# Order edges for side work on TensorE, and new VectorE durations in the account that paces it

## The chip, the cores and the metric

One core of a Trainium2 chip runs the whole kernel. The metric is the device time of one execution in microseconds; a kernel's time is the median over several runs. Engines are named as in the profile: PE is TensorE's matmuls and PEld its weight loads, DVE is VectorE, ACT is ScalarE, POOL is GpSimd, SP is SyncE, which issues most DMAs.

## The reference

One layer of a streaming encoder, on 2048 prompt frames and 64 sample frames, 1024 channels, all in fp32:

```python
h = rms_norm(x, p['norm1_g']) * (1 + sc1) + sh1
z = h @ p['w_in']
glu_a, glu_b, q, k, v, g_conv, g_attn = jnp.split(z, offs, axis=-1)
u = glu_a * jax.nn.sigmoid(glu_b)
conv_out, conv_state = conv_module(u, conv_hist, ...)   # 31 taps, LayerNorm, swish, projection
q, k = rms_norm per head
o = attend(q, k, v, p['rel_bias'])                       # own chunk of 64 and 8 before, 8 heads
attn_out = o @ p['w_attn_out']
merged = jax.nn.sigmoid(g_conv) * conv_out + jax.nn.sigmoid(g_attn) * attn_out
x = x + gt1 * (merged @ p['w_o'])
h2 = rms_norm(x, p['norm2_g']) * (1 + sc2) + sh2
gate, up = jnp.split(h2 @ p['w_ffn_in'], 2, axis=-1)
x = x + gt2 * ((jax.nn.silu(gate) * up) @ p['w_ffn_out'])
```

`sh1`, `sc1`, `gt1` and so on come from a projection of a conditioning vector. The outputs are both parts' frames, the convolution's last 30 rows, and new keys and values.

## The kernel before

Every fp32 product is done as three matmuls on values split into a high and a low part (`mm3`: high by high, high by low, low by high). ScalarE makes the high part, VectorE or GpSimd the low one by subtraction.

**Two phases.** The first (to about 1211 us in the trace) runs over four blocks of some 512 frames. For each block, in the order `q`, GLU columns 0, `k`, GLU columns 1, `v`, GLU columns 2 and 3, `g` (16 columns of gates), TensorE does the main line of products: `qkv`, `glu`, `gates`. The second phase runs over three token blocks with the merge, the output projection, the residual and the feed-forward part.

**Side work.** Beside the main line runs work that is written as Python generators and held in lanes: `norm_tile` and `cached_kv` (the next block's normalised and transposed input), `qk_rows` (norm and transposition of q and k rows), `attend` (one head of attention: scores `sc`, VectorE's row maximum, ScalarE's exponential, transpositions `ptp`, products `po`), `conv_norm` (the convolution's LayerNorm, whose means are matmuls `pm`) and `convolve` (30 VectorE steps a channel tile). Their order of precedence is `[norm_lane, work, attn, tail, conv]`. A generator yields the time at which its next step may be emitted.

**The account.** `Meter` wraps each engine. Every instruction that is traced adds an assumed duration to `Stream.load` of its engine; nothing of it is measured while the kernel is built. TensorE's sum is the clock. After each product (`mm3`, `mm2`) at least 500 ns of that clock on, `tick` lets each lane emit a step if the time that it yielded has come and no engine is further ahead of TensorE than the lane's room: `CONV_ROOM = 2000` ns of VectorE for the convolution, `ATTN = {"dve": 3000, "act": 4000}` for attention, 2500 ns between the score tiles of one head. The waits are built from `stream.when(...)`, the account of the engine whose result is needed, plus lags such as `PE_LAG = 400`, `MEAN_LAG = 10000` (before `conv_norm`, except in the last block) and `KN_LAG = 5000`.

**Drains.** At fixed places a lane is emptied, whatever its times say: `conv.drain()` and `tail.drain()` at GLU stage 0 of each block (so the norm of a block must be through by then), `norm_lane.drain` of a tile ahead of its q product, and `attn`, `conv` and `tail` at the end of the first phase. At the eleventh gate of the last block the convolution is drained too.

**Emission and issue.** Emission fixes the order in which instructions are traced. The framework's scheduler then orders each engine's queue by what it reckons ready, so that an instruction can be issued ahead of one traced before it. `tc.issue_after(x)` gives all instructions of x's engine that are traced in its block an order edge behind x: issue order alone, no wait for x to end. Before the change it is used on VectorE, around single steps.

**The second phase** has lanes of its own (`turns`, `work`), made after the first ones are gone; its weight handling (`Weights`) uses the same account, for when a buffer is given up and whether GpSimd or VectorE makes a low part.

All instructions go through one helper line of `Meter`, L105, so the profile's rows are told apart by tile names.

Of the kernel before, what the change touches and what calls it, by code (L numbers as in the profile page):

```python
# [87 lines left out]
class Meter:  # L88


    def __init__(self, engine, name, stream):
        self.engine, self.name, self.stream = engine, name, stream

    def __getattr__(self, op):
        f = getattr(self.engine, op)
        if op == "dma_start":
            return f

        def run(*args, **kw):
            out = kw.get("out", args[0] if args else None)  # L100
            n = 1
            for d in out.shape[1:]:
                n *= d
            self.stream.add(self.name, op, n, args, kw)
            return f(*args, **kw)  # L105

        return run


class Lane:  # L110

# [4 lines left out]
    def add(self, gen):  # L118
        self.gens.append([gen, 0.0, {}])
# [6 lines left out]
        self.step(self.gens[-1])  # L126

    def step(self, entry):
        try:
            got = next(entry[0])  # L130
        except StopIteration:
            self.gens.remove(entry)
            return
        entry[1], entry[2] = got if isinstance(got, tuple) else (got, {})
# [28 lines left out]
class Stream:  # L163
# [1 line left out]


    def __init__(self):
        self.lanes, self.later, self.last = [], [], 0.0
        self.load = {"pe": 0.0, "dve": 0.0, "act": 0.0, "pool": 0.0}

    def add(self, name, op, n, args, kw):
        if name == "pe":
            x = args[1]
            if op == "transpose":
                ns = 128 / 1.2
            elif x.dtype == F32:
                ns = max(n, 64) / (2.4 if "tile_position" in kw else 0.6)
            else:
                ns = (n if n >= 256 else 512) / 2.4
        elif name == "act":  # L180
            ns = 220 + 0.83 * n
        elif name == "pool":
            ns = 260.0 * n if ALU.pow in args else 60 + 2.25 * n
        else:
            fast = op in ("tensor_scalar", "tensor_copy")
            ns = 75 + n * (8.3 if op == "reciprocal" else 0.75 if fast else 1.04)
        self.load[name] = max(self.load[name], self.load["pe"]) + ns

    def full(self, room):
# [401 lines left out]
def streaming_layer(ctx: ExitStack, tc: tile.TileContext, I, O):  # L591
    nc = tc.nc
    stream = Stream()
    pe, dve, act, gps = (
        Meter(e, n, stream) for e, n in ((nc.tensor, "pe"), (nc.vector, "dve"), (nc.scalar, "act"), (nc.gpsimd, "pool"))
    )
# [959 lines left out]
    attn = Lane(ATTN, ATTN_NS, wide=2)  # L1556
    conv, tail = Lane({"dve": CONV_ROOM}, burst=4), Lane({})
    stream.lanes = [norm_lane, work, attn, tail, conv]

    hh = wk.tile([P, KT, QB + SMP], F32R, tag="hh", name="hh")  # L1560
    hl = wk.tile([P, KT, QB + SMP], F32R, tag="hl", name="hl")
# [224 lines left out]
    for s, (lo, hi) in enumerate(CBLOCKS):  # L1786
# [214 lines left out]
        def up(f, ops, at):  # L2001
# [12 lines left out]
            if not f:  # L2014
                z = bank("y")
                step(z, "s3", "t3", True, False)
            step(y, "s2", "t2", f < EARLY, False)
            rest_of_late(1)
            u2 = piece("t1", "u2")[:, :half]
# [4 lines left out]
            if f:  # L2024
                z = bank("y")
                step(z, "s3", "t3", True, False)
# [185 lines left out]
```

## Time and profile before

| | |
|---|---|
| median of 3 runs | 3004.08 us (2999.04 to 3005.18) |
| the profiled execution | 2997.87 us, span 2995.2 us |
| TensorE busy | 2910.2 us, 97% |
| weight loads | 2595.7 us, 87% |
| VectorE busy | 2030.2 us, 68% |
| ScalarE, GpSimd | 1324.2 us, 942.1 us |
| granted TensorE clock, mean | 0.991 |
| end of the first phase | 1211 us |

The page's first part gives each engine's busy time. A row of the waits reads: who waited, for whom, total us, times, longest. A row of the timeline reads: start, duration, engine, line, operation, output and inputs, shapes, count, and in brackets the idle time before it and what ended it. A row of the windows reads: from and to, length, each engine's busy time with its count of instructions, the granted clock as a share of full speed, the DMA engines' busy share and GB/s. In names of tiles, `sc`, `ptp`, `po` are attention, `pm` the convolution's norm, `pt` transpositions, `ps` the main line's products, `y<-u,wd,y` a convolution step.

### The profile page before, as it was taken

To read this page: it belongs to the slowest core of one execution; us is meant where nothing else is said; L and a number is where in the kernel's file an instruction comes from. 1 tells how busy PE (TensorE), PEld (TensorE's weight loads), DVE (VectorE), ACT (ScalarE), POOL (GpSimd) and SP (SyncE) were. 2 spreads that over 40 slices of the span, in tenths; PEclk is the share of its full clock that TensorE was granted. 3 is DMA by queue.
4 is the path that set the end of the run, shared out by engine and by line. 5 is a ranking of instruction groups with operands and counts; after the bars stand their busy time and mean duration, and the time that the engine had idled before them with its cause. 6 is when DMAs were issued, how large, how long until landed. Compare 5 with 4: busy or idle time off the path is not lost.

```text
span 2995.2 us, 44652 instructions
## 1 busy us (share of the span) xinstructions
PE 2910.2 (97%) x16199; PEld 2595.7 (87%) x16199; DVE 2030.2 (68%) x3661; ACT 1324.2 (44%) x2375; POOL 942.1 (31%) x597
## 2 busy tenths in 40 slices
PE   7999989999999999989999999999999999999999
PEld 4888867887888788888999999999999898999998
DVE  5878688677866895577777755556566757366567
ACT  3344642463366257464444345434444244333332
POOL 1200120011011102355455433256656441333333
PEclk9999999999999999999999999999999999999999
DMA  8888889878987788886444786446556955355545
GB/s 299 272 290 270 290 263 304 277 251 273 306 283 248 251 268 289 267 287 235 146 153 161 253 282 230 138 141 204 189 177 213 360 197 190 117 168 176 169 155 186
DMA packets 487017, 690.95 MB, mean 231 GB/s; under 512 B 38420, under 2 KB 316808, under 8 KB 486797
## 3 DMA queue, kind: packets, MB, share of 16 engines
q1 hardware_dynamic: 469749, 662.07, 66.9%
q10 hardware_dynamic: 17048, 26.04, 2.4%
q8 instruction: 127, 2.08, 0.3%
q14 instruction: 93, 0.76, 0.1%
HBM read 503.79 MB, written 184.19 MB: 230 GB/s over the span
## 4 chain that ended last, share of the span: by engine, by line
PE 84%; DVE 8%; DMA 4%; issue 1%; POOL 1%; ACT 1%; SPq 0%; ACTq 0%; DVEq 0%; POOLq 0%
PE ps L105 55%; PE pd L105 14%; PE pw L105 6%; DVE y L105 3%; PE sc L105 2%; PE po L105 2%; PE ptp L105 2%; PE pt L105 1%; POOL r L105 1%; DVE wlo L105 1%; PE pa L105 1%; DMA wlo<-w_dfi_l 1%; DMA out<-acc 0%; DMA g_d<-gate 0%; DMA kk<-k_d 0%
## 5 line engine op out<-in xcount | busy, mean ns | idle before, releaser
L105 POOL TENSOR_TENSOR wlo<-wst,whi 128x1024 fp32r<-128x1024 f32 (+1 forms) x167 | 382.7, 2295 | 566.6 <-ACT whi L105 491.5
L105 PE MATMUL ps<-t,whi 128*128 128x384 f32 (+1 forms) x2112 | 506.0, 323 | 10.2 <-DVE t L105 6.2
L105 PE MATMUL pd<-whi,hid 128*128 128x512 f32 x1356 | 440.3, 391 | 2.7 <-DVE acc L105 2.7
L105 ACT ACTIVATE whi<-wst 128x1024 fp32r<-128x1024 f32 (+1 forms) x271 | 265.0, 982 | 376.8 <-PE ps L105 126.1
L105 PEld LDWEIGHTS ps<-t,whi 128*128 128x128 f32 x2112 | 369.7, 188 | 19.7 <-DVE t L105 7.8
L105 PE MATMUL ps<-b,whi 128*128 128x384 f32 (+1 forms) x1584 | 380.1, 326 | 4.4 <-DVE pt L105 2.4
L105 DVE SCALAR_TENSOR_TENSOR y<-u,wd,y 128x512 f32<-128x512 f32 (+1 forms) x480 | 369.2, 772 | 7.7
L105 PE MATMUL ps<-hh,whi 128*128 128x512 f32 (+2 forms) x992 | 364.8, 368 | 0.0
L105 PE MATMUL ps<-hl,whi 128*128 128x512 f32 (+2 forms) x992 | 347.7, 351 | 0.0
L105 PE MATMUL ps<-hh,wlo 128*128 128x512 f32 (+2 forms) x992 | 347.2, 350 | 0.0
L105 PE MATMUL ps<-t,wlo 128*128 128x384 f32 (+1 forms) x1056 | 340.1, 322 | 0.0
L105 DVE TENSOR_TENSOR acc<-acc,pd 128x512 f32<-128x512 f32 x440 | 289.7, 683 | 65.9 <-PE pd L105 62.3
L105 PEld LDWEIGHTS pd<-whi,hid 128*128 128x128 f32 x1356 | 254.5, 188 | 56.9 <-DVE acc L105 5.1
L105 PEld LDWEIGHTS ps<-b,whi 128*128 128x128 f32 x1584 | 277.4, 189 | 6.1 <-DVE pt L105 2.7
L105 PE MATMUL pd<-wlo,hid 128*128 128x512 f32 x700 | 273.8, 391 | 0.0
L105 PE MATMUL ps<-b,wlo 128*128 128x384 f32 (+1 forms) x792 | 256.6, 324 | 0.0
L105 ACT ACTIVATE pr<-pr,sm 128x640 f32<-128x640 f32 (+3 forms) x272 | 199.9, 746 | 121.6 <-DVE sm L105 117.7
L105 PEld LDWEIGHTS ps<-hh,wlo 128*128 128x128 f32 x992 | 188.3, 190 | 23.6 <-issue 1.2
L105 PEld LDWEIGHTS ps<-hh,whi 128*128 128x128 f32 x992 | 188.8, 190 | 20.0 <-issue 4.1
L105 PEld LDWEIGHTS ps<-hl,whi 128*128 128x128 f32 x992 | 189.2, 191 | 16.0 <-issue 2.5
L105 POOL TENSOR_TENSOR r<-t,mhalf 128x1 f32<-128x1 f32 (+3 forms) x68 | 82.0, 1208 | 378.2 <-DVE t L105 367.1
L105 PEld LDWEIGHTS ps<-t,wlo 128*128 128x128 f32 x1056 | 198.6, 188 | 0.9
(220 smaller groups left out, 5664.7 us busy)
## 6 DMA issues: line engine op xcount, KB each, us to landing
whi<-w_din_h SPq DMA_DIRECT2D x72, 512.0 KB, 5.6
wlo<-w_din_l SPq DMA_DIRECT2D x72, 512.0 KB, 7.6
wst<-sum_d SPq DMA_DIRECT2D x132, 256.0 KB, 3.0
wmod<-in_w_ada SPq DMA_DIRECT2D x48, 512.0 KB, 6.2
sum_d<-ws SPq DMA_DIRECT2D x88, 256.0 KB, 2.2
wst<-in_w_ffn_in SPq DMA_DIRECT2D x84, 256.0 KB, 3.2
wst<-in_w_in SPq DMA_DIRECT2D x40, 512.0 KB, 5.9
wst<-in_w_ffn_in SPq DMA_DIRECT2D x37, 512.0 KB, 5.5
```

Source lines behind the costliest of these rows:

```text
L105: return f(*args, **kw)
```

## The change

Two things are changed. First, `Meter` notes the last TensorE instruction traced (`stream.latest`), and `Lane.step` runs each step of a generator of the five lanes of the first phase inside `issue_after` of it. `Lane.stream` is set for those five lanes alone; lanes made later have none and run as before. Second, the account's VectorE durations are replaced: instead of 75 ns and 1.04 ns an element (0.75 for `tensor_scalar` and `tensor_copy`, 8.3 for `reciprocal`), each kind has a base and a rate of its own.

```diff
             self.stream.add(self.name, op, n, args, kw)
-            return f(*args, **kw)
+            one = f(*args, **kw)
+            if self.name == "pe":
+                self.stream.latest = one
+            return one
...
 class Lane:
+
+    stream = None
...
     def step(self, entry):
+        one = self.stream.latest if self.stream is not None else None
         try:
-            got = next(entry[0])
+            with self.stream.tc.issue_after(one.ins) if one is not None else nullcontext():
+                got = next(entry[0])
...
-            fast = op in ("tensor_scalar", "tensor_copy")
-            ns = 75 + n * (8.3 if op == "reciprocal" else 0.75 if fast else 1.04)
+            base, each = {
+                "tensor_scalar": (300, 0.45), "tensor_copy": (300, 0.45), "reciprocal": (75, 8.3),
+                "scalar_tensor_tensor": (220, 1.04), "tensor_tensor_reduce": (230, 1.04),
+            }.get(op, (150, 1.04))
+            ns = base + each * n
...
     stream.lanes = [norm_lane, work, attn, tail, conv]
+    stream.tc = tc
+    for lane in stream.lanes:
+        lane.stream = stream
```

`either`, which chooses between VectorE and GpSimd for a few operations, keeps the old figures, and its margins (`TT_LESS = 9e9`) leave them all on VectorE.

More of the change, by code (lines that the diff above doesn't have):

```diff
@@ L167, in __init__ @@
     def __init__(self):
-        self.lanes, self.later, self.last = [], [], 0.0
+        self.lanes, self.later, self.last, self.latest = [], [], 0.0, None
         self.load = {"pe": 0.0, "dve": 0.0, "act": 0.0, "pool": 0.0}
```

## The prediction

> **What bounds the kernel now.** I read the page first, then who waited for whom on TensorE (PE) up to the second phase, then busy times stage by stage.
>
> ```profile
> span 2995.2 us, 44652 instructions
> PE 2910.2 (97%) x16199; PEld 2595.7 (87%) x16199; DVE 2030.2 (68%) x3661; ACT 1324.2 (44%) x2375; POOL 942.1 (31%) x597
> ```
>
> TensorE is the bound: 85 us of the span are idle on it. A change of order can win those, and what the clock loses around them, and no more; VectorE (DVE) has a third of the span free. TensorE's waits between 60 and 600 us (total, times, longest):
>
> ```profile
> PE pm L105 <- POOL s L105: 9.2, 1, 9.2
> PE sc L105 <- DVE sm L105: 8.6, 6, 3.2
> PE ptp L105 <- ACT pr L105: 7.9, 5, 4.0
> PE pt L105 <- DVE kn L105: 2.9, 2, 1.8
> ```
>
> All four are side work: `pm` is the convolution's norm, `sc` and `ptp` are attention, `pt<-kn` the turning of q and k rows. Together 28.6 us. Columns below: window, PE, PEld, DVE, ACT, POOL busy, granted clock, DMA. The windows are: k and v rows and the GLU columns of the second block, the same of the third block, the third block's gates, and the last block's gates.
>
> ```profile
> 400.00:525.00 125.00, 116.89 (x624) 90.27 (x613) 104.40 (x197) 42.87 (x88) 9.32 (x11) 0.96 0.88 289
> 682.00:796.00 114.00, 112.61 (x626) 91.73 (x628) 89.72 (x153) 33.43 (x60) 11.88 (x11) 1.00 0.90 299
> 796.00:926.00 130.00, 130.00 (x741) 110.17 (x734) 91.83 (x184) 75.06 (x135) 13.16 (x14) 1.00 0.86 275
> 1068.00:1211.00 143.00, 140.41 (x752) 118.96 (x750) 101.43 (x199) 95.25 (x165) 21.92 (x14) 1.00 0.82 262
> ```
>
> The third block has almost no stall, the second block loses 8.1 us to idle time in the same stages. So there is something to win in the first 600 us, and something to lose after them.
>
> **Part one: pinning.** During a step of a side lane, each TensorE instruction gets an order edge behind the last TensorE instruction traced before the step. It is no wait, and instructions of other engines and DMAs get no edge. It binds only where the scheduler had moved side work ahead; the lanes of the second phase get none. The clear place in the trace:
>
> ```profile
> 502.63 8.40 DMA whi<-w_din_h
> ```
> ```profile
> 508.03 0.74 PE L105 MATMUL sc<-kk,q 128*128 128x320 f32 x4
> 511.95 1.43 PE L105 MATMUL sc<-kk,q 128*128 128x320 f32 x4 [3.17 <-DVE sm L105]
> 514.31 1.43 PE L105 MATMUL sc<-kk,q 128*128 128x320 f32 x4 [0.93 <-DVE sm L105]
> 516.67 1.44 PE L105 MATMUL sc<-kk,q 128*128 128x320 f32 x4 [0.93 <-DVE sm L105]
> 519.04 0.80 PE L105 MATMUL ps<-hh,whi 128*128 128x512 f32 x1
> ```
>
> Four score tiles of one head stand together, the last three ahead of the gates' first matmuls, and each waits until VectorE has emptied the bank of the one before. The step that issues a score tile was emitted between gate matmuls, so the edges spread them out again. That takes away 3.17 + 0.93 + 0.93 = 5.03 us, but not all of it is won: the gates' weights, issued at 502.63, land 8.40 later at 511.03, and the score tiles before end at 508.77, so TensorE stands 2.3 us either way. Net -2.7 us. The clock:
>
> ```profile
> 113.00:115.20 2.20, 0.38 (x3) 0.11 (x2) 0.91 (x2) 0.00 (x0) 1.26 (x1) 1.00 0.00 0
> 115.30:118.70 3.40, 3.40 (x14) 2.81 (x13) 1.98 (x6) 3.04 (x7) 1.65 (x1) 0.51 0.42 91
> 508.70:511.30 2.60, 0.07 (x1) 0.00 (x0) 2.42 (x5) 0.00 (x0) 0.21 (x1) 1.00 1.05 406
> 511.30:521.50 10.20, 7.70 (x29) 4.82 (x29) 9.90 (x22) 6.57 (x12) 0.00 (x0) 0.50 0.45 158
> ```
>
> After the stall the clock is at one half for 10.2 us, 7.70 of them busy, which costs 7.70 / 2 = 3.9 us. A wait of 1.8 us (2.20 less 0.38 busy) at 113 was followed by 3.4 us at one half, or 1.7 us lost, so a 2.3 us stall keeps about that much: -2.2 us of the clock at best; I take -1.5, and -0.8 for the other score waits of the table (8.6 less 5.03). Part one: **-5 us**. Ends: 0 (the scores come to wait elsewhere) and -10 (the weights' landing moves too).
>
> [...]
>
> **Part two: VectorE's account.** The account paces the lanes: convolution steps are emitted while VectorE is at most 2000 ns ahead of TensorE, attention at 3000, and each `yield` of a time waits for VectorE's count. Durations (busy, mean ns, idle before) up to 1211 us:
>
> ```profile
> L105 DVE SCALAR_TENSOR_TENSOR y<-u,wd,y 128x512 f32<-128x512 f32 x360 | 268.4, 749 | 6.1
> L105 DVE SCALAR_TENSOR_TENSOR y<-u,wd,y 128x606 f32<-128x606 f32 x120 | 100.8, 844 | 1.6
> L105 DVE TENSOR_TENSOR pl<-ptp,ph 128x512 fp32r<-128x512 f32 x128 | 86.6, 687 | 58.4 <-ACT ph L105 57.2
> L105 DVE CUSTOM_DVE_ANT_0 pr<-sc,bias 128x640 f32<-128x640 f32 x96 | 78.5, 818 | 24.1 <-PE sc L105 23.7
> ```
>
> Old formula against new: a convolution step 607 and 752 ns (705 and 850 at 606 wide), a 512 wide tensor_tensor 607 and 682, a row maximum 741 and 896, a 128 wide tensor_scalar 171 and 358. Those of the rows are the mean durations now. But as a rate a duration counts too much, since the next instruction starts before the last one ends:
>
> ```profile
> 361.71 0.69 DVE L105 TENSOR_TENSOR hl<-h,hh 128x512 fp32r<-128x512 f32 x1
> 362.32 0.68 DVE L105 TENSOR_REDUCE ssq<-sq 128x8 f32<-128x512 f32 x1
> ...
> 511.07 0.82 DVE L105 CUSTOM_DVE_ANT_0 pr<-sc,bias 128x640 f32<-128x640 f32 x1
> 511.81 0.08 DVE L105 DVE_READ_ACCUMULATOR2_ANT sm<- 128x1 f32 x1
> ```
>
> Start to start it is 0.61 and 0.74 us, the old 607 and 741. So the old account was right for these and short for the convolution; the new one is right for the convolution and long for the rest. In the third block's gates the program's formulas give VectorE 81.8 us before and 99.0 us after (44 steps of +145, 44 tensor_tensor of +75, 20 maxima of +155, 16 small tensor_scalar of +187), against 121.0 us of TensorE: shares of 0.68 and 0.82. The trace has 91.83 of 130.00, or 0.71. The lanes will believe in a VectorE fuller than it is, and emit side work later. Where that lands, place by place:
>
> First 600 us: attention and q/k rows, emitted later, find their inputs ready more often, and fewer convolution steps stand ahead of a row maximum. Of the table's 28.6 us, `pm` (9.2) and the three score waits (5.03) are counted elsewhere; 14.4 us remain, with some 4 us of half clock (an estimate, two stalls at the 1.7 us of the row at 113). I take well under half: **-7 us**. Ends 0 and -18.
>
> The norm of the first block. Its convolution needs, in the new account, 105.8 us; what the other VectorE work leaves in the stages up to the gates (each stage's TensorE time less that work) is 47.6, so 58.2 go into the gates, where 60.1 of 119 us are free. It ends 115 us into them instead of 71 (the same sum with the old formulas gives 68). Then come the norm's fixed 10 us and 46 us of its small part, and the deadline is 29 us after the gates: the next block's first GLU stage drains the lane at once. Today this happens with the large part alone:
>
> ```profile
> 379.36 2.60 POOL L105 TENSOR_TENSOR s<-s,ln 128x512 f32<-128x512 f32 x2 [9.34 <-ACT ln L105]
> 384.84 2.08 PE L105 MATMUL pm<-s,ones 128*128 128x512 f32 x2 [9.24 <-POOL s L105]
> 385.93 1.42 PE L105 MATMUL ps<-hh,whi 128*128 128x512 f32 x1
> ```
>
> Then half of the small part and the three sums on POOL (2.60 / 2 = 1.3 us each, 3.9) join that chain, in front of `pm` and of the columns. 3.9 for the sums and 4 for the rest of the small part (an estimate: somewhat under half of the 9.24 us that one such chain costs today): **+8 us**. Ends 0 (columns are issued in between) and +14.
>
> The turn into the next block (the next q rows, window as above):
>
> ```profile
> 338.00:374.00 36.00, 33.54 (x166) 25.65 (x165) 23.65 (x71) 20.50 (x53) 6.54 (x5) 1.00 0.83 263
> ...
> 926.00:959.00 33.00, 33.00 (x181) 27.96 (x180) 25.25 (x62) 22.09 (x45) 6.33 (x5) 1.00 0.61 186
> ```
>
> The first turn loses 2.5 us today, the last nothing. In blocks two and three 47 convolution steps instead of 41 are left for the gates, 35 us at a free share of 0.56: they end 63 us into the gates instead of 36, and the norm behind them runs on into the turn, where it shares VectorE with the next block's tiles, whose eight small tensor_scalar are priced 1.5 us more per tile. I take 1 us for each of three turns: **+3 us**, ends 0 and +9.
>
> The end of phase one. Attention of the last block ends with the last gate:
>
> ```profile
> 1208.67 0.27 PE L105 MATMUL po<-pl,vv 128*128 128x128 f32 x1
> 1211.41 0.87 PE L105 MATMUL ps<-cin,whi 128*128 128x320 f32 x2 [2.47 <-DVE o_p L105]
> ```
>
> A head has 4 maxima and some 6.5 tensor_tensor in its chain: +1.1 us on the 33 us that a head takes in the account with two in flight, 3.4%, or 4 us over the account's 131 us of this stage, and up to 9 where the other head's are in the way too. That much is left for the drain when no gate matmul covers it; `DVE pl` alone has 5 x 0.69 there, and the convolution's norm, 12 us later by the same sum as above, adds its tail. **+7 us**; ends 0 (the steps' grain swallows it) and +12.
>
> Phase two has no pinned lane; the residual tiles are emitted later, and drains wait for more. Its waits on such tiles today, in the same view from 1211 us on:
>
> ```profile
> PE ps L105 <- DVE t L105: 6.8, 5, 2.4
> ...
> PE pw L105 <- ACT xn L105: 2.7, 1, 2.7
> ```
>
> Three sections of about 1 us: **+3 us**, ends -5 and +8. No DMA is added or removed; weight loads and stores are queued on SP by the same events, later by tenths of a microsecond, which I price at nothing since the third block shows TensorE uncovered for 0.0 us in its gates.
>
> **Sum.** -5 - 7 + 8 + 3 + 7 + 3 = +9 us. The profiled execution took 2997.87 us (2995.2 of span and 2.7 around it), 6.2 under the median of 3004.08, so +9 gives 3007 beside it and **3013 us** as the median. One measurement of this kernel can tell about 0.2%, or 6.0 us, from no change: faster is under 2998.1, slower over 3010.1.
>
> **Rivals.** (a) Faster: the smoothing wins and the drains do not cost. What decides is the order at the first drain: if the scheduler issues the columns at 385.93 ahead of a `pm` that it knows to be late, the +8 is 0, and with -5, -7 to -18 and half of the last three terms (+6) the time is 3004 - 6 to 3004 - 17, with 2992 in the middle. For it: 28.6 us of waits of just the kind that a longer account removes. Against it: the scheduler left TensorE 9.24 us before `pm` with columns ready behind. (b) The change does not do what it says: few edges bind, since most side work already stands behind the main line, and later emission shifts stalls without changing their sum: -5 + 5 = 0, 2999 to 3009 us. For it: only the scores near 512 us show a cost of running ahead. (c) A worse slow case, inside the forecast: all upper ends at once, 14 + 9 + 12 + 8 = +43 with nothing won, 3047; they share causes, but hardly all.
>
> **Chances.** Slower, as summed: 0.41, its own range 3010 to 3040. Faster (a): 0.35. Same (b): 0.24. The range over all cases leaves out about a tenth on each side: of the fast case the times below 2982, where nearly all of -5 and -18 would have to come with no drain paid; of the slow one those above 3038, about four fifths of the upper ends' 43.
>
> **What would show it.** Right: score tiles no longer grouped before 519; convolution steps of the first block still running near 338 us (end of the gates); the wait of `pm` on POOL grown beyond 9.2 us; attention's `po` after the last gate matmul with more than 2.47 us before `ps<-cin`. Wrong: `pm` not waiting at all, phase one ending before 1205 us, or new stalls inside the third block's gates, for which I charged nothing.

## The result, and the profile after

The changed kernel takes 3082.34 us in the median (3080.84 to 3083.43); the kernel before, run beside it, 3004.63 us. The ratio is 1.0267, with a 95% interval of [1.0252, 1.0281]: slower by some 78 us, where 9 were forecast. The profiled execution's first lines:

```profile
span 3079.1 us, 44630 instructions
PE 2925.9 (95%) x16199; PEld 2607.3 (85%) x16199; DVE 2143.7 (70%) x3786; ACT 1324.7 (43%) x2375; POOL 719.6 (23%) x472
```

TensorE has the same 16199 instructions and 15.7 us more busy time (2910.2 before); its mean granted clock is 0.981 instead of 0.991, so I read the 15.7 us as clock lost around stalls. The rest of the 83.9 us between the two spans is idle time: 153.2 instead of 85.0. VectorE has 125 instructions more and GpSimd 125 fewer. That is something the diff does not say in words, and it becomes important below. Who TensorE waited for, over the whole span (total, times, longest):

```profile
PE pm L105 <- POOL s L105: 28.7, 4, 14.9
PE ps L105 <- DVE t L105: 14.9, 6, 9.8
PE sc L105 <- DVE sm L105: 13.1, 11, 4.5
PE ptp L105 <- ACT pr L105: 9.9, 7, 4.9
```

The four kinds of the forecast's first list are all there (`pt<-kn` with 5.0 us stands just below these rows), and none of them is smaller than before. To see where time went, take three instants that both traces have: the first column matmul after the first drain (`ps<-hh,whi` behind `pm`), the last gate matmul, and the first matmul of the second phase (`ps<-cin`).

| stretch | before | after | difference |
|---|---|---|---|
| start to the columns behind the first drain | 385.9 | 406.7 | +20.8 |
| from there to the last gate matmul | 822.1 | 827.2 | +5.1 |
| last gate matmul to phase two | 3.4 | 29.0 | +25.6 |
| phase two | 1783.8 | 1816.2 | +32.4 |

An instant also moves with the side work that was done ahead of it, so the first row has to be read with the matmuls in it, before and after:

```profile
0.00:385.93 385.93, 345.47 (x2149) 295.15 (x2149) 277.59 (x564) 172.65 (x363) 46.95 (x60) 0.97 0.85 284
```
```profile
0.00:406.71 406.71, 342.12 (x2101) 293.33 (x2102) 270.76 (x536) 162.07 (x336) 47.24 (x60) 0.92 0.81 267
```

The changed kernel has 48 matmuls fewer behind it at that instant, 24.1 us more idle time (64.6 and 40.5) and a lower clock, so up to there it has lost more than the 20.8 us of the table. Of the idle time 19.4 us more lie at the drain itself (28.7 from 373.5 us on, 9.2 from 374 us on before) and 3.9 in the turn ahead of it.

The first drain, in TensorE's timeline of the changed kernel; it answers to the single wait of 9.24 us before:

```profile
388.33 0.69 PE L105 MATMUL pm<-s,ones 128*128 128x64 f32 x2 [14.86 <-POOL s L105]
390.96 0.69 PE L105 MATMUL pm<-s,ones 128*128 128x64 f32 x2 [1.94 <-POOL s L105]
397.49 2.07 PE L105 MATMUL pm<-s,ones 128*128 128x512 f32 x2 [5.84 <-POOL s L105]
405.63 2.08 PE L105 MATMUL pm<-s,ones 128*128 128x512 f32 x2 [6.07 <-POOL s L105]
406.71 1.42 PE L105 MATMUL ps<-hh,whi 128*128 128x512 f32 x1
```

All four means of both parts' norms (64 columns and 512 columns wide) stand there. What they wait for is in VectorE's queue, and behind it in GpSimd's:

```profile
376.45 11.45 DVE L105 SCALAR_TENSOR_TENSOR y<-u,wd,y 128x606 f32<-128x606 f32 x13
```
```profile
387.99 0.29 POOL L105 TENSOR_TENSOR s<-s,y 128x64 f32<-128x64 f32 x1 [9.21 <-DVE y L105]
```

Thirteen convolution steps in one run of 11.45 us: the convolution itself had not ended when the drain came.

The end of phase one and the first merge, TensorE:

```profile
1233.94 0.39 PE L105 MATMUL ps<-hh,wlo 128*128 128x512 f32 x1
...
1262.89 0.56 PE L105 MATMUL ps<-cin,whi 128*128 128x320 f32 x2 [1.40 <-DVE o_p L105]
...
1280.00 0.90 PE L105 MATMUL ps<-cin,whi 128*128 128x320 f32 x2 [9.80 <-DVE t L105]
```

And by windows (length, busy times of PE, PEld, DVE, ACT, POOL, granted clock, DMA): the stretch between last gate and phase two, and phase two, with phase two of the kernel before under it.

```profile
1234.40:1262.89 28.49, 18.52 (x88) 14.16 (x86) 16.19 (x29) 16.48 (x30) 5.93 (x4) 0.76 0.34 98
1262.89:3079.10 1816.21, 1761.68 (x9688) 1634.16 (x9688) 1255.13 (x2064) 753.25 (x1291) 571.96 (x326) 0.99 0.60 197
```
```profile
1211.41:2995.20 1783.79, 1755.35 (x9688) 1630.05 (x9688) 1136.40 (x1928) 749.60 (x1283) 796.65 (x450) 1.00 0.60 200
```

Behind the last gate stand 88 matmuls of attention; TensorE is idle for a third of that time and has a clock of 0.76. In phase two TensorE does the same 9688 matmuls, but VectorE is busy 118.7 us longer and GpSimd 224.7 us shorter. The groups that make the low parts of weights say why; GpSimd before, then both engines after (count, busy, mean ns, idle time before them):

```profile
L105 POOL TENSOR_TENSOR wlo<-wst,whi 128x1024 fp32r<-128x1024 f32 (+1 forms) x167 | 382.7, 2295 | 566.6 <-ACT whi L105 491.5
```
```profile
L105 POOL TENSOR_TENSOR wlo<-wst,whi 128x1024 fp32r<-128x1024 f32 (+1 forms) x101 | 238.6, 2365 | 659.6 <-ACT whi L105 499.9
L105 DVE TENSOR_TENSOR wlo<-wst,whi 128x1024 fp32r<-128x1024 f32 (+1 forms) x180 | 214.6, 1198 | 139.1 <-ACT whi L105 127.7
```

`Weights.split` gives a low part to VectorE when GpSimd's account is more than `BEHIND` = 4000 ns ahead of TensorE's. GpSimd's account waits for ScalarE's and that for VectorE's, so VectorE's longer durations push GpSimd's up too (so the code reads; no run takes it apart). Over all low parts of phase two the emission has 165 on GpSimd and 306 on VectorE after, 290 and 181 before: VectorE, believed slower, gets some 125 pieces more to do.

### The profile page after: what moved, and what is told of

The parts are those of the page before. It is cut to its first block, busy times and chain, and to the rows that moved or that the text cites. A ratio compares the mean times of both kernels' runs of the same rounds, so it can differ in the third digit from the quotient of the medians.

```text
span 3079.1 us, 44630 instructions
## 1 busy us (share of the span) xinstructions
PE 2925.9 (95%) x16199; PEld 2607.3 (85%) x16199; DVE 2143.7 (70%) x3786; ACT 1324.7 (43%) x2375; POOL 719.6 (23%) x472
## 4 chain that ended last, share of the span: by engine, by line
PE 48%; DVE 2%; DMA 1%; issue 1%; ACT 1%; POOL 0%; SPq 0%; DVEq 0%; POOLq 0%; ACTq 0%
PE ps L105 30%; PE pd L105 14%; PE pw L105 4%; DVE wlo L105 1%; ACT whi L105 0%; DVE acc L105 0%; DMA wst<-in_w_attn_out 0%; DMA cin<-c_d 0%; DVE pd L105 0%; DMA wst<-in_w_ffn_in 0%; POOL acc L105 0%; POOL ws L105 0%; DVE t L105 0%; DVE pw L105 0%; PE pt L105 0%
## 5 line engine op out<-in xcount | busy, mean ns | idle before, releaser
L105 POOL TENSOR_TENSOR wlo<-wst,whi 128x1024 fp32r<-128x1024 f32 (+1 forms) x101 | 238.6, 2365 | 659.6 <-ACT whi L105 499.9
L105 DVE TENSOR_TENSOR wlo<-wst,whi 128x1024 fp32r<-128x1024 f32 (+1 forms) x180 | 214.6, 1198 | 139.1 <-ACT whi L105 127.7
L105 PEld LDWEIGHTS ps<-hh,whi 128*128 128x128 f32 x992 | 189.5, 191 | 22.5 <-issue 3.1
```

Of the source, the lines that this page charges most:

```text
L105: one = f(*args, **kw)
```

## The experiments

The theory after the traces: the edges are not the loss, the durations are, and at three separate places: the first drain, the end of phase one with the first merge behind it, and the choice of engine in phase two. Rivals: the edges lose it; the places are one delay that wanders; any later emission costs the same wherever it is.

All runs, with the instants from each one's trace (before: 385.9, 1211.4, 1783.8):

| kernel | median us | ratio to before, 95% | columns at | phase two at | phase two lasts |
|---|---|---|---|---|---|
| the change | 3082.34 | 1.0267 [1.0252, 1.0281] | 406.7 | 1262.9 | 1816.2 |
| e1 edges only | 2998.53 | 0.9996 [0.9987, 1.0005] | 387.0 | 1212.6 | 1783.2 |
| e2 durations only | 3058.32 | 1.0190 [1.0173, 1.0207] | 396.0 | 1234.0 | 1825.0 |
| e3 old in phase two | 3055.13 | 1.0186 [1.0171, 1.0201] | 401.6 | 1253.8 | 1796.2 |
| e4 old to the first drain | 3051.56 | 1.0166 [1.0145, 1.0187] | 387.8 | 1239.7 | 1813.1 |
| e5 old in the last block | 3049.35 | 1.0159 [1.0143, 1.0176] | 406.1 | 1247.2 | 1801.0 |
| e6 old choice of engine | 3069.61 | 1.0233 [1.0211, 1.0256] | 407.1 | 1256.9 | 1799.4 |
| e7 before, new choice | 3017.79 | 1.0059 [1.0043, 1.0075] | 386.6 | 1214.6 | 1803.7 |
| e8 distances as durations | 3041.08 | 1.0134 [1.0106, 1.0161] | 391.8 | 1234.4 | 1796.9 |
| e9 e1 without edges in the last gates | 2988.41 | 0.9961 [0.9948, 0.9973] | 386.3 | 1203.7 | 1782.9 |
| e10 old at all three places | 2990.10 | 0.9960 [0.9948, 0.9972] | 384.7 | 1204.1 | 1782.5 |
| e11 change without edges in the last gates | 3074.30 | 1.0236 [1.0220, 1.0253] | 403.7 | 1251.7 | 1820.3 |
| e12 e10 without edges in the last gates | 2990.01 | 0.9959 [0.9946, 0.9973] | 387.5 | 1207.0 | 1785.8 |

One caution for the table: e3, e6 and the change have the same program up to phase two, and their instants there spread by 9 us (1253.8 to 1262.9). The medians and their intervals carry the verdicts; an instant tells where, not to the microsecond how much.

**e1, the edges alone.** The account's formula as before, the edges as in the change.

```
-            base, each = {...}.get(op, (150, 1.04))
-            ns = base + each * n
+            fast = op in ("tensor_scalar", "tensor_copy")
+            ns = 75 + n * (8.3 if op == "reciprocal" else 0.75 if fast else 1.04)
```

> The order edges with the old VectorE durations, so that the same instructions are emitted in the same order as before the change and only the issue order on TensorE differs. If the new durations cost the 78 us (theory): 2995 to 3008 us, a gain of 0 to 9 us, the three score waits near 512 us (5.0 us together) gone. If the edges cost it, because side work that is held behind the main line comes too late (rival): above 3040 us.

No difference: 0.9996. It is the sum of two. At the second block's gates the stall before 512 us is gone; the row of the kernel before, then the stretch that answers to it with edges, which stands 10 us earlier:

```profile
500.00:530.00 30.00, 24.97 (x124) 17.63 (x123) 24.54 (x45) 9.45 (x17) 1.66 (x3) 0.83 0.77 256
```
```profile
490.00:520.00 30.00, 29.63 (x180) 21.90 (x179) 28.51 (x51) 8.93 (x16) 0.42 (x2) 1.00 1.01 334
```

The clock is back at 1.00, and the gates begin 9.9 us earlier than before (509.16 and 519.04). In the last block's gates 8.5 us are lost again, at one score tile that waits for a row maximum, and at the half clock behind it:

```profile
1080.70 1.44 PE L105 MATMUL sc<-kk,q 128*128 128x320 f32 x4 [4.79 <-DVE sm L105]
```
```profile
1080.70:1085.30 4.60, 4.59 (x17) 4.01 (x17) 3.56 (x8) 2.31 (x5) 0.00 (x0) 0.50 0.52 211
```

At this half clock matmuls of 512 columns start 0.42 and 0.43 us apart (from 1081.94 us on), ahead of the wait 0.22 to 0.23 us. 4.79 us of wait and 4.59 / 2 = 2.3 us of clock are 7.1 of the 8.5; two waits for `kk` of 1.8 us together make up most of the rest.

**e9, the same without the edges in the last gates.** The lanes are let go before that stage:

```
     for b, stage in ORDER:
         lo, hi = PBLOCKS[b]
+        if (b, stage) == (3, "g"):
+            for lane in stream.lanes:
+                lane.stream = None
```

> The edges alone with the old durations, and without the edges in the last block's gates (its lanes are unpinned from there on). The edges alone took 9.5 us off at the second block's gates and put 8.5 us on in the last block's gates. Theory one (the two are separate events, each local): the first stays and the second goes, so 8 to 9 us less than the kernel before, about 2992 us. Rival (the loss in the last gates is the price of the gain, work of the attention that has to be done in any case): within 3 us of the kernel before.

Theory one, with somewhat more than the 8 to 9 us expected: 13 us off the time of the kernel before (2988.41 against 3001.48 beside it). Gain and loss of e1 are separate events. The stage in e1 and in e9, from 1061 us to the end of phase one:

```profile
1061.00:1212.00 151.00, 142.49 (x750) 120.72 (x748) 99.01 (x198) 95.26 (x165) 20.70 (x14) 0.98 0.79 246
```
```profile
1061.00:1204.00 143.00, 140.26 (x751) 119.12 (x750) 100.96 (x198) 95.31 (x166) 21.55 (x14) 1.00 0.84 261
```

Same work, 8 us apart, of which 5.8 idle (8.51 and 2.74) and 2.2 clock.

**e2, the durations alone.**

```
-        one = self.stream.latest if self.stream is not None else None
+        one = None
```

> The new VectorE durations without the order edges. Theory: 3075 to 3095 us, as slow as the changed kernel or somewhat slower, with 88 matmuls of attention still to be issued after the last gate column as there. Rival (edges): near 3004 us. If the two parts only cost together: well under 3050 us here and in the run with the edges alone.

1.0190: most of the loss comes without a single edge, though the time is under the range that the theory gave. But the change has 1.0267, and edges alone do nothing: on top of the new durations they cost another 0.0077 x 3004 = 23 us. The two parts do not add.

**e4, the old durations up to the first drain.** Both formulas in the account, and a switch:

```
     for b, stage in ORDER:
+        stream.old = (b, stage) in ORDER[: ORDER.index((1, 0))]
```

> The changed kernel, with the old durations in the account up to the first drain (the start of the second block's first GLU quarter) and the new ones from there on. The first convolution's work is then issued ahead of the drain as before, 20 norm operations of VectorE are left there instead of 37. Theory one (the work left at the first drain costs its ~24 us there): the second block's first GLU stage starts no later than before, the wait pm<-POOL s is back near 9 us or below, and the time is 3082 - 20..24 = 3058 to 3062 us. Rival (the delay there is swallowed later, since the kernel has to do the same work anyway): the time stays at 3075 to 3084 us.

The drain is as it was, and the time is 30 us lower (1.0267 - 1.0166, times 3004; so in all that follows), more than the 20 to 24 expected:

```profile
386.74 2.08 PE L105 MATMUL pm<-s,ones 128*128 128x512 f32 x2 [8.61 <-POOL s L105]
387.83 1.42 PE L105 MATMUL ps<-hh,whi 128*128 128x512 f32 x1
```

The rival, that the delay would be swallowed later, is out. Nothing later in the kernel takes up the 20 us that TensorE lost at 390: phase two starts 23.2 us earlier (1239.7). Not all of the 30 us lies at the drain, though. The columns start 18.9 us earlier with 48 matmuls more behind them, and the gap behind the last gate, which the edit does not touch, is 22.5 us instead of 29.0.

**e5, the old durations in the last block of phase one** (`stream.old = b == 3`, and new again in phase two).

> The changed kernel, with the old durations in the account in the last block of phase one alone, the new ones before it and in phase two. Behind the last gate 24 attention matmuls are then left instead of 88 (4 in the kernel before). Theory one (what is left behind the last gate costs the ~25 us between the last gate and phase two): the gap between the last gate matmul and phase two's first shrinks from 29 us to 8 to 14 us, and the time is 3082 - 15..25 = 3057 to 3067 us. Rival (the attention's matmuls have to be done somewhere, and pushing them under the gates costs the same there): 3075 to 3084 us, with the last block's stages longer by what the gap loses.

```profile
1241.41 0.39 PE L105 MATMUL ps<-hh,wlo 128*128 128x512 f32 x1
...
1247.22 0.57 PE L105 MATMUL ps<-cin,whi 128*128 128x320 f32 x2 [1.40 <-DVE o_p L105]
```

The gap is 5.8 us instead of 29.0, less than the 8 to 14 expected, and the time is 32 us lower, 8 us under the expected range. Part of what the rival said is true: the last gates themselves get 7 us longer (last gate matmul at 1241.4 instead of 1233.9), so by the instants only 15.7 us come from phase one. The other 15 come from phase two (1801.0 instead of 1816.2), some 11 of them in the first merge: the last block's norm is no longer left over there. In the changed kernel 12 VectorE operations of it are still to be issued behind the last gate, and they run into the first merge. VectorE there, in the changed kernel:

```profile
1276.35 0.69 DVE L105 TENSOR_TENSOR part_l<-ln,part_h 128x512 fp32r<-128x512 f32 x1 [4.33 <-DMA c_d<-part_l]
1279.46 0.49 DVE L105 SCALAR_TENSOR_TENSOR t<-tg,ps 128x320 f32<-128x320 f32 x1 [2.42 <-DMA c_d<-part_l]
```

The norm's `part_l` waits 4.33 us, by the profile for the store of an earlier `part_l`. The merge's `t` comes behind it in the same queue, waits another 2.42 us, and TensorE waits 9.80 us for it at 1280.00.

**e3, the old durations in phase two alone** (`stream.old = True` ahead of it), **e6, the old choice alone**, and **e7, the new choice in the kernel before.** In e6 and e7 the account is untouched, and the slabs that the other kernel gave to VectorE are written down as a list:

```
-        if name == "pool" and self.sum_pool and self.stream.load["pool"] - self.stream.load["pe"] > BEHIND:
+        if name == "pool" and self.sum_pool and i in ON_DVE:
```

> The changed kernel, but from the start of the second phase on the account uses the old VectorE durations. In the changed kernel the first phase ended 51.5 us later and the second took 32.4 us longer. If the second phase loses by its own pricing: about 3082 - 30 = 3052 us (3045 to 3058), with the first phase ending near 1263 us. If it loses because the late first phase leaves it a bad start (convolution norm and attention drained into it): 3075 us or more.

> The changed kernel, but each weight slab's low part in phase two is made on the engine that the kernel before chose (290 on GpSimd, 181 on VectorE, instead of 165 and 306). Theory one (the choice of engine is what phase two loses): phase two gives back 18 to 22 us, the waits ps<-DVE t fall, and the time is about 3062 us. Rival (VectorE is late in phase two because side work is issued at other places, whoever makes the low parts): 3078 to 3084 us.

> The kernel before with one thing changed: the low parts of the second phase's weights are made on the engine that the changed kernel's account chose for each (113 of 414 slabs go from GpSimd to VectorE, 15 the other way). Emission times are those of before. If the choice of engine makes the second phase slow: 3004 + 20 to 30 us, 3024 to 3034. If the late emission of the residual tiles makes it slow: 3004 us within 5.

e7 is the cleanest: only the engine of the low parts differs (some 125 more on VectorE) from the kernel before, and it is slower by 1.0059, or 17.5 us, less than the 20 to 30 expected, all of it in phase two (1803.7 against 1783.8 us). Its waits there:

```profile
PE ps L121 <- DVE t L121: 21.0, 11, 7.9
```

The kernel before has 6.8, 5, 2.4 in that row (the list in e7 moves the line numbers). How VectorE stood ahead of low parts, for whom, us and times, in the kernel before and in e7:

```profile
  ACT whi L105: 86.1, 47
```
```profile
  ACT whi L121: 164.7, 100
```

A low part is weight minus high part, and the high part is made by ScalarE. On GpSimd, what stands behind a low part that waits for ScalarE (491.5 us in the row of the kernel before above) is low parts and sums above all (17 short steps of the norm, `r`, are made there too; ScalarE's `xn` waits 7.3 us for them in all of phase two, before). On VectorE it is the residual, the norm and `t`, for which TensorE waits (21.0 us in e7). So although the operation takes 1.2 us there and 2.3 to 2.4 us on GpSimd, the faster engine makes the kernel slower.

That the choice costs 17.5 us is shown. By which of two ways is not: VectorE stands 78.6 us longer for ScalarE in e7, but it is also busy 106.9 us longer in all (2137.1 and 2030.2), and a longer queue delays `t` too. The longest wait speaks for the second. In TensorE's timeline of e7, then by windows over the length of that wait:

```profile
1332.65 0.82 PE L121 MATMUL ps<-b,whi 128*128 128x288 f32 x2 [7.94 <-DVE t L121]
```
```profile
1324.71:1332.65 7.94, 0.01 (x1) 0.03 (x1) 7.94 (x20) 4.53 (x11) 1.69 (x2) 0.80 1.01 349
```

VectorE is busy through the whole wait. In the 50 us up to its end (from 1283) it makes 19 low parts and stands 5.5 us for ScalarE ahead of them; in the 47 us that answer to them in the kernel before (1278.4 to 1325.7) it makes 8 and stands 4.7 us.

e6 gave 10 us (13 by the medians) where about 20 were expected; in its trace phase two lasts 1799.4 us, 16.8 shorter than in the change. e3, with the old account in all of phase two, has 1796.2, 20.0 shorter. Both keep the bad first merge of about 10 us, which lies in phase two but comes from phase one.

**e10, the old durations at all three places.**

```
     for b, stage in ORDER:
+        stream.old = b == 3 or (b, stage) in ORDER[: ORDER.index((1, 0))]
...
+    stream.old = True
```

> The changed kernel with the old durations at all three places where it lost: up to the first drain, in the last block of phase one, and in phase two; the new durations stay for the second and third block only, the edges stay. Undoing them one at a time took 31 us, 33 us and 27 us off the changed kernel's time, 91 us together, where the whole loss against the kernel before is 78 us. Theory one (the three losses are local and add up): 2991 to 3002 us, the kernel before or a little better. Rival (each undoing is worth less once the others are done, as 36 attention matmuls are still left behind the last gate, 4 in the kernel before): 3010 to 3025 us.

2990.10 us: theory one, just under its lower end. Undone one at a time the three gave, by ratios, 0.0101 (e4), 0.0108 (e5) and 0.0081 (e3), 0.0290 or 87 us together; undone together they give 0.0307, or 92 us. Within the intervals the losses add up. What is left, the edges and the new durations in the second and third block, is faster than the kernel before: 0.9960. But e9, which has none of the new durations, has 0.9961, so no run shows that the new durations win anything by themselves.

**e11 and e12, where the edges cost with the new durations.** Both let the lanes go in the last gates as e9 does, e11 in the changed kernel, e12 in e10.

> The changed kernel with its new durations, without the edges in the last block's gates and behind them. With the new durations the edges cost 24 us more than without edges (3082 against 3058 us), with the old durations nothing. Theory one (the edges keep the attention that is issued late, 88 matmuls behind the last gate, from being moved up between the gates): the gap ahead of phase two gets shorter by 8 to 15 us and the time is 3067 to 3074 us. Rival (the extra cost of the edges lies in the blocks before, at the first drain above all): 3078 to 3084 us.

> The kernel with the old durations at the three places, and also without the edges in the last block's gates: new durations for the second and third block only, edges up to the last block's third GLU quarter. If both corrections hold (the losses of the three places add up, and the loss of the edges in the last gates goes): 2983 to 2993 us, faster than the kernel before by 0.3 to 0.6%. Rival (36 attention matmuls behind the last gate cost 10 us or more, which takes back the gain): 2998 to 3010 us.

e11 gains 0.0031 or 9 us of the 23, and at 3074.3 us it just misses the range of theory one. The mechanism of theory one does not hold: the gap behind the last gate is 25.3 us (1226.4 to 1251.7) instead of 29.0, not 8 to 15 us shorter, and the same 88 matmuls stand in it. What is gone is a wait inside the gates, of this score tile in the changed kernel:

```profile
1183.19 0.61 PE L105 MATMUL sc<-kk,q 128*128 128x320 f32 x1 [5.52 <-DMA whi<-w_din_h]
```

The other 14 us lie before the last gates: these begin at 1091.2 in e11 and at 1070.9 in e2, which has no edges at all (at the first drain the changed kernel has its columns at 406.7, e2 at 396.0). No run takes them apart. e12, at 2990.01, lies where theory one put it, but it gains nothing over e10 (2990.10): with the old durations in the last block of that kernel the edges in the last gates cost nothing that could be won back. So the 8.5 us of e1 belong to how the work falls there, and are no fixed price of edges in that stage.

**e8, the account by distances.** VectorE's formula set to the time from one start to the next, of instructions that follow each other without a wait, in place of durations:

```
-                "tensor_scalar": (300, 0.45), "tensor_copy": (300, 0.45), ...
-                "scalar_tensor_tensor": (220, 1.04), "tensor_tensor_reduce": (230, 1.04),
-            }.get(op, (150, 1.04))
+                "tensor_scalar": (260, 0.45), "tensor_copy": (260, 0.45), ...
+                "scalar_tensor_tensor": (220, 1.04), "tensor_tensor_reduce": (75, 1.04),
+            }.get(op, (75, 1.04))
```

> The changed kernel with VectorE's account set to the start-to-start distance of instructions that follow each other (260 + 0.45 n for copies and tensor_scalar, 220 + 1.04 n for scalar_tensor_tensor, 75 + 1.04 n for the rest) in place of their durations; the edges stay. In the emission that puts 289 low parts of phase two on GpSimd and 182 on VectorE as before, leaves 32 norm operations at the first drain (37 in the changed kernel, 20 before) and 28 attention matmuls behind the last gate (88, and 4). Theory one (a duration includes time in which the next instruction already runs, so the account counts too much work and puts side work off): most of the loss is gone, 3020 to 3035 us, still slower than before by the drain and the end of phase one. Rival (any correction of the account upwards costs the same, because the thresholds were fitted to the old one): 3060 us or more.

3041.08 us: half of the loss is gone (1.0134 instead of 1.0267), but the range of theory one was missed by 6 us. The first drain costs little (391.8), the gap behind the last gate is 6.5 us, phase two is 1796.9 us with the old choice of engine. One new event was not foreseen, 18 convolution steps in one run in the last block, with a score tile behind it; VectorE's row, then TensorE's:

```profile
1060.49 14.14 DVE L105 SCALAR_TENSOR_TENSOR y<-u,wd,y 128x512 f32<-128x512 f32 x18
```
```profile
1073.08 1.41 PE L105 MATMUL sc<-kk,q 128*128 128x320 f32 x4 [10.16 <-DVE y L105]
```

So an account that is nearer to the measured distances loses less than one of durations, and still loses 1.3% against the old one. The thresholds beside it (2000 ns of room for the convolution, 10000 ns ahead of its norm, 4000 ns `BEHIND`) were left as they were; whether other thresholds would make the better account win was not tried.

## Why the prediction was wrong

The direction and most of the places were right. The terms were not: the sum had +9, the spans differ by 83.9.

- **Pinning, -5.** The mechanism was right and larger than forecast: the score tiles stand between the gates' matmuls in the changed kernel's trace, and e1's gates begin 9.9 us earlier. I had kept 2.3 us of stall for the landing of the weights, and half clock with it; e1 shows neither (29.63 us busy of 30.00 around its gates' start, clock 1.00). But the end of the range that I set at 0, "the scores come to wait elsewhere", is what happened: 8.5 us in the last gates. Alone the part measures -1.8 us with an interval that includes nothing (e1); with the last gates left out, -13 (e9).
- **The half clock.** The stall of 2.3 us, which I priced by the row at 113 (1.8 us of wait, then 3.4 us at 0.51), did not come about, and e1's stall of 4.8 us was followed by 4.6 us at 0.50. But phase two of the kernel before has two waits of about that length, 2.37 us up to 1885.48 and 2.41 us up to 2519.62; each wait, then what followed, for the first after 1.4 us at full clock:

```profile
1883.00:1885.50 2.50, 0.13 (x2) 0.03 (x1) 2.50 (x4) 1.06 (x1) 0.14 (x1) 1.00 0.48 153
1886.90:1890.20 3.30, 3.30 (x12) 2.92 (x11) 3.30 (x6) 0.71 (x2) 0.00 (x0) 0.50 0.62 171
...
2517.20:2519.60 2.40, 0.01 (x1) 0.00 (x0) 2.40 (x4) 1.06 (x1) 0.08 (x1) 1.00 0.50 169
2519.60:2523.00 3.40, 2.67 (x14) 2.35 (x15) 3.40 (x6) 1.58 (x3) 0.00 (x0) 1.00 0.57 189
```

  Half clock (0.50 for 3.3 us) followed the first and not the second (1.00). So of these three waits, 1.8, 2.37 and 2.41 us, two had half clock behind them and one had not: the half clock that I kept for a stall of 2.3 us was one of two outcomes.
- **First 600 us, -7.** In the stretch from 400 to 525 us, TensorE is idle for 8.1 us in the kernel before, for 2.2 in e9 (edges, no new durations) and for none in e10. So most of what is won there is the edges', and the smoothing that this term stands for won some 2 us there. In the changed kernel 19 of the 20.8 us lost at the first drain are back by the second block's gates, the pinning's 9.9 among them, but in part because work is put off and not saved: from there on each stretch from a block's first columns to its gates is longer (130.7 us instead of 114.3 in the third block, 124.8 instead of 109.2 in the last). The third block's, after and before:

```profile
680.90:811.57 130.67, 129.18 (x740) 105.62 (x738) 106.50 (x196) 58.82 (x100) 17.77 (x16) 1.00 0.95 314
```
```profile
682.10:796.40 114.30, 112.91 (x630) 91.67 (x628) 90.12 (x153) 33.33 (x59) 11.88 (x11) 1.00 0.90 299
```

  It holds 110 matmuls more and has the same idle time (1.5 and 1.4 us): a shift, no loss.
- **The norm of the first block, +8, ends 0 and 14.** Measured +20.8 by the instants, and +19.4 by the idle time at the drain alone. The failing step is "It ends 115 us into them instead of 71": by it the convolution was through 4 us ahead of the gates' end (119 us) and 33 us ahead of the drain. In the emission 15 of its steps and all 37 VectorE operations of both norms (20 before) were left to the drain; the trace has those steps from 374.21 us on, 13 of them in the run above. The sum gave the steps all of VectorE's free time; that they stand last in the order of precedence and so did not get it is how I read the code, and no run shows it. e4 shows that this work, issued ahead of the drain as before, costs nothing. And "half of the small part" was all of it, with the convolution in front.
- **The turns, +3, ends 0 and +9.** They cost somewhat more than the upper end: TensorE is idle in the three turns for 6.4, 3.6 and 2.8 us instead of 2.5, 0.1 and 0.0, some 10 us more. The later two are shorter all the same, since they hold fewer matmuls. The second, after and before:

```profile
650.80:680.90 30.10, 26.52 (x134) 21.23 (x132) 22.40 (x50) 19.54 (x39) 8.56 (x7) 1.00 0.49 145
```
```profile
648.20:682.10 33.90, 33.85 (x186) 28.60 (x184) 25.59 (x62) 22.73 (x46) 6.33 (x5) 1.00 0.62 191
```

- **The end of phase one, +7, ends 0 and 12.** Measured 25.6, and some 10 more in the first merge. The failing step is the price of a head's chain: 3.4% of one head. As I read it, an account that runs ahead delays each step of each head by its whole excess and not by one head's chain; what the emission shows is 88 matmuls left, where there were 4. The sign that I gave, more than 2.47 us before `ps<-cin`, was wrong in the same way; that wait is 1.40, and the time lies in the attention ahead of it.
- **Phase two, +3, ends -5 and +8.** Measured 32.4. The failing step is that the sum priced only waits for residual tiles, about 1 us a section. Its largest part was not in the sum at all: `Weights` reads the same account to choose an engine. e7 prices that at 17.5 us; some 10 more are the first merge, which comes from phase one. I looked for what the durations delay and not for everything that reads them.
- **The third block's gates, nothing.** Right: 129.13 us busy of 130.00 there in the changed kernel.
- **The two parts together.** I added them. They interact by 23 us. Edges hold work where it was traced, and with the new durations it is traced late, which is how I read it; e11 has 9 of the 23 in the last gates and the gap behind them; the rest is not taken apart.

One reading of the durations was wrong: the row maximum is priced at 896 ns and its row has 818. The row that I quoted to say that a duration counts too much was the right warning. A tensor_tensor of 512 columns, priced at 682 ns by the new formula, has a duration of 0.69 us in the trace and a distance of 0.61 (at 361.71 us, before). e8 against the change, 3041 against 3082 us, is what an account by distances is worth here, all thresholds being equal.

## What to carry to other kernels

Before a constant of a planner is corrected, list everything that reads it, the choices of engine above all, and find the places where work that it puts off has no cover left: a drain, the end of a phase, a queue with something urgent behind it. A truer duration alone can lose when the thresholds beside it stay as they were. In this kernel it cost nothing where work still had room behind it, in the second and third block (e10), and it won nothing there either (e9). The order edges paid where the scheduler had pulled work ahead into a wait, and cost where they held work back: e9, which leaves them out of the last gates, is faster than both kernels (0.9961 [0.9948, 0.9973]), and so is e10.

## What the runs showed of the hardware that was not expected

Moving an operation to the engine that does it in half the time cost 17.5 us (e7): a low part of 1024 columns takes 1.22 us on VectorE there and 2.40 us on GpSimd, in the median. On VectorE it stands ahead of work for TensorE, with its wait for ScalarE's result (86.1 us in all before and 164.7 in e7) and with its own time (106.9 us more in all); which of the two costs more is open. The durations favour VectorE; the kernel's time goes the other way.

During the whole first drain of the changed kernel, from 385 to 408 us, the granted clock was at one half, which costs 5.82 / 2 = 2.9 us beside the idle 17.2:

```profile
385.00:408.00 23.00, 5.82 (x10) 2.75 (x11) 12.19 (x25) 9.80 (x21) 9.73 (x15) 0.50 0.06 12
```

Convolution steps that follow each other without a wait take 11.45 / 13 = 0.88 us at 606 columns and 14.14 / 18 = 0.79 us at 512, so their distance is no shorter than their duration (0.844 and 0.749 in the mean before), while a tensor_tensor's distance is 0.08 us shorter than its duration. So in this account a correction by durations is right for the convolution steps and wrong for a tensor_tensor. Each of these steps reads the `y` that the one before it wrote; whether that, or the kind of operation, makes the difference is not shown.
